# A list scheduler that gets TensorE's work in runs, at other prices

## The chip, the cores and the metric

The kernel runs on one core of a Trainium2 chip. Its engines are TensorE (PE in the profile; its weight loads are PEld), VectorE (DVE), ScalarE (ACT), GpSimd (POOL) and SyncE (SP), which issues the DMAs. Each engine works through its own instructions in order. The metric is the device time of one execution in microseconds, as the median of three runs.

## The reference

Two transformer blocks of two layers each on 256 tokens of width 1024, in float32. The first block has a gated delta rule beside an mLSTM in its first layer (`mixer_ab`) and windowed attention in its second (`mixer_c`), each followed by a feed-forward with squared relu of width 4096 and a gated per-layer input. The second block has five attentions side by side in each layer and a gated feed-forward of width 2816 with a short convolution:

```python
for layer in range(DEPTH):                       # first block
    mix = mixer_ab(hn, ...) if layer % 2 == 0 else mixer_c(hn, ...)
    h = h + rmsnorm(mix, gains[1])
    ff = jnp.square(jax.nn.relu(hn @ w_up[layer])) @ w_down[layer]
    h = h + rmsnorm(ff, gains[3])
    h = h + jax.nn.sigmoid(h @ w_ple_gate[layer]) * (p[layer] @ w_ple[layer])
...
for l in range(DEPTH):                           # second block
    mixed = jnp.concatenate([_merge(o_a), ..., _merge(o_e)], axis=-1)
    x = x + mixed @ w_o[l]
    x = x + (jax.nn.silu(gate) * (xn @ ffn_w_up[l])) @ ffn_w_down[l]
```

## The kernel before, in words

**Products in three passes.** A float32 product is made of three float32r products: high part of the activations times high part of the weights, and the two mixed products with a low part. `block` loads a weight block of 1 MB by DMA into a `raw` tile (two buffers) and splits it into `hi` and `lo` (four buffers each) in four parts: `hi` is a copy on ACT or DVE, `lo` is a subtraction on DVE.

**Two forms.** `tmm` (line 748) has the weights stationary and 256 tokens moving: for each of 2 channel groups and 8 k-tiles three matmuls of 256 columns, 48 for a block, all into one PSUM bank. `nmm` (line 760) has the activations stationary (one of two token tiles) and 512 columns of weights moving; for one k-tile and two banks it gives the six matmuls pass by pass, the two banks alternating:

```python
for i, b in enumerate(banks):
    pe.matmul(b[:, :n], a[0], hi[:, i * n : (i + 1) * n], start=first, stop=False)
for i, b in enumerate(banks):
    pe.matmul(b[:, :n], a[0], lo[:, i * n : (i + 1) * n], start=False, stop=False)
for i, b in enumerate(banks):
    pe.matmul(b[:, :n], a[1], hi[:, i * n : (i + 1) * n], start=False, stop=last)
```

In a feed-forward `tmm` makes the hidden units of block u, and `nmm` adds those of block u-1 into four banks that stay open (24 matmuls for a block: two token tiles, two k-tiles, two banks, three passes). There are 16 such blocks in each layer of the first block and 11 in each of the second, where `tmm` runs twice for a block. `transposes` (line 870) puts 2 to 4 transposes of 128x128 into one bank.

**The planner.** Nothing is issued as the program names it. `Recorder.note` (line 335) takes each instruction down as an `Op` with its price and with the instructions that it must follow because their data overlap; for PSUM a whole bank counts as one piece, so that matmuls into a bank keep their order. `price` (line 378) gives a time in ns by engine and size. For PE it is 118 for a transpose, 2 + 0.417 n for n columns of float32r or bfloat16, and 2 + max(1.67 n, 212) for float32. `arrange` (line 454) then lays the instructions out in time with these prices: at each step the engine that can start first gets, among what it can start first, the instruction with the highest rank, that is, the longest way to the end by `tails` (line 400). A tile of a pool is taken ahead of its turn only where the program's own order still fits. `order` (line 428) goes through seven such layouts and keeps the one with the shortest planned time. `issue` (line 568) emits the instructions in that order; every engine's queue follows from it. All instructions in the profile therefore carry line 571. Which of two engines makes a copy (ACT or DVE) or a column operation (POOL or DVE) is also decided in `arrange`, by what can end sooner.

A norm's factor is computed by `rsqrt_of` on POOL and DVE in a chain of small steps; `to_aT` transposes normed rows and splits them into `aTh` and `aTl`, which all following products read.

Of the kernel before, what the change touches and what calls it, by code (L numbers as in the profile page):

```python
# [36 lines left out]
# ---------------------------------------------------------------- layout of small inputs  # L37
# [35 lines left out]
# ---------------------------------------------------------------- constants of the shapes  # L73
# [66 lines left out]
def layout(x):  # L140
# [64 lines left out]
    def setk(name, g, n):  # L205
        """the gain of n heads below each other; of keys, one column for each head alone"""
        if COLS[name][1] == 1:
            return setc(name, np.tile(g, n))
        z = np.zeros((n, g.size, n), f32)
        for i in range(n):  # L210
            z[i, :, i] = g
        setc(name, z.reshape(P, n))
# [43 lines left out]
class Op:  # L256
    __slots__ = ("eng", "call", "args", "kwargs", "cost", "lag", "preds", "succs", "tiles", "table", "rank", "alt")
# [9 lines left out]
class Recorder:  # L267
    """Takes the program's instructions down in the order in which it names them, and issues them in another:
    each engine gets, of what can start first, the instruction with the longest way to go. Every order of two
    instructions on overlapping data is kept, and a pool's tile is taken ahead of its turn only if the  # L270
    program's own order still fits into the pool from there on."""
# [8 lines left out]
    def __init__(self, nc):  # L280
        self.engines = {"pe": nc.tensor, "act": nc.scalar, "dve": nc.vector, "pool": nc.gpsimd, "sp": nc.sync}
        self.ops, self.pools, self.tile_pool, self.seen = [], {}, {}, {}

    # ---------------------------------------------------------------- taking down
# [9 lines left out]
    def new(self, pool, bufs, tile):  # L294
        """a tile of a pool that is used again"""
# [4 lines left out]
    def either(self, first, second):  # L300
        """an instruction for the engine that can do it sooner; (engine, call, operands, keywords) each"""
# [7 lines left out]
    def copy(self, out, src, scale=1.0):  # L309
        """out = scale * src on ScalarE or VectorE"""  # L310
# [6 lines left out]
    def scalar(self, *args, **kwargs):  # L317
        """tensor_scalar of a column on GpSimd or VectorE"""
        self.either(("pool", "tensor_scalar", args, kwargs), ("dve", "tensor_scalar", args, kwargs))

    def box(self, x):
        """(tile, partitions, columns) of an operand; None if it isn't on the chip"""
# [12 lines left out]
    def note(self, eng, call, args, kwargs):  # L335
        op = Op()
        op.eng, op.call, op.args, op.kwargs = eng, call, args, kwargs
        op.preds, op.succs, op.tiles, op.alt = {}, [], [], None
# [8 lines left out]
        i = len(self.ops)  # L347
# [4 lines left out]
        self.ops.append(op)  # L352
# [25 lines left out]
    def price(self, op, out, ins):  # L378
        """a rough time in ns"""
# [4 lines left out]
        if op.eng == "pe":  # L384
            if op.call == "transpose":
                return 118
            n = _size(ins[1])
            return 2 + 0.417 * n if ins[1].dtype in (F32R, BF16) else 2 + max(1.67 * n, 212.0)
# [10 lines left out]
    # ---------------------------------------------------------------- putting in order  # L399
    def tails(self, starts):  # L400
        """each instruction's time to the end when the program is laid out from its end backwards"""
# [44 lines left out]
    def swap(self, op):  # L446
        """the other form of an instruction"""
# [6 lines left out]
    def arrange(self):  # L454
# [33 lines left out]
        p0, gone, out = 0, [False] * n, []  # L488
        by_rank, top = sorted(range(n), key=lambda i: -ops[i].rank), 0
        while len(out) < n:  # L490
# [4 lines left out]
            for e, cand in avail.items():  # L495
                pick = None
                for i in cand:
# [8 lines left out]
                    ok = True  # L506
                    for t in op.tiles:
                        if t not in taken:
                            p = pool[t]
                            room = self.pools[p] - (KEEP.get(p, 0) if op.rank < lead - SLACKTIME else 0)  # L510
                            if first[t] > p0 and use[p][p0 : first[t]].max() >= room:
                                ok = False
                                break
                            at = max(at, min(s[e] for s in slots[p]))
# [29 lines left out]
            for t in op.tiles:  # L544
                p = pool[t]
                if t not in taken:
# [21 lines left out]
    def issue(self):  # L568
        for i in self.order():
            op = self.ops[i]  # L570
            getattr(self.engines[op.eng], op.call)(*op.args, **op.kwargs)  # L571


class Loom:
    """Chains of dependent steps, each taken as far as what it needs is there."""
# [36 lines left out]
    def until(self, ready, *keys):  # L612
        """within a chain: wait for keys in ready"""
# [5 lines left out]
def program(ctx, tc, A, out, dbg=None):  # L619
# [64 lines left out]
    # ------------------------------------------------------------ resident data  # L684
# [33 lines left out]
    def pick(row):  # L718
        """as lhsT: that row of the moving operand on every output partition"""
        return ident[:, row : row + 1].to_broadcast([P, P])  # L720

    # ------------------------------------------------------------ weights
    def block(name, i, k, w):
        """block i of a packed weight: high and low parts [P, k, w]"""
# [11 lines left out]
    def whole(name, i, k, w):  # L736
        """block i of a packed weight as it is, for float32 products: four passes, but nothing to prepare"""
# [9 lines left out]
    # ------------------------------------------------------------ matrix products  # L747
    def tmm(bank, hi, lo, n=2):
        """bank[:, j, tokens] = (channel group j of the block)^T @ aT"""
        for j in range(n):  # L750
            c = ts(j)
            o = bank[:, j, :]
            for k in range(8):
                pe.matmul(o, hi[:, k, c], aTh[:, k, :], start=(k == 0), stop=False)
                pe.matmul(o, hi[:, k, c], aTl[:, k, :], start=False, stop=False)
                pe.matmul(o, lo[:, k, c], aTh[:, k, :], start=False, stop=(k == 7))
                if k % 4 == 3:
                    loom.step()

    def nmm(banks, a, hi, lo, first, last, n=512):  # L760
        """banks (column halves of n) += act^T @ W for one k-tile"""
        for i, b in enumerate(banks):
            pe.matmul(b[:, :n], a[0], hi[:, i * n : (i + 1) * n], start=first, stop=False)
        for i, b in enumerate(banks):
            pe.matmul(b[:, :n], a[0], lo[:, i * n : (i + 1) * n], start=False, stop=False)
        for i, b in enumerate(banks):
# [1315 lines left out]
```

## Time and profile before

| | |
|---|---|
| median of 3 runs | 1451.15 us (1449.95 to 1454.01) |
| span of the profiled execution | 1450.2 us |
| PE busy | 1401.3 us (97%), 8856 matmuls |
| PEld / DVE / ACT / POOL busy | 1239.8 / 1000.2 / 796.1 / 199.9 us |
| mean granted clock of PE | 0.994 of full speed |
| DMA | 236.40 MB, 163 GB/s in the mean |

The span is from the first to the last instruction. Busy time is the time in which an engine works at one instruction at least. A matmul's duration in the profile includes its passage through the array; matmuls follow each other faster than that, so their pace is read from starts that follow each other. A row of several instructions shows the time from the first start to the last end. A window counts an instruction that reaches into it from before as well.

### The profile page before, as it was taken

What the parts mean: (1) busy time and instruction counts of PE and PEld (TensorE: products, weight loads), DVE (VectorE), ACT (ScalarE), POOL (GpSimd) and SP (SyncE); (2) the same over time, 40 slices, a digit from 0 to 9 for tenths busy, and PEclk for the clock granted to TensorE, in tenths of its full rate; (3) what the DMA queues carried; (4) which work ended last, traced back from release to release, by engine and by line L of the source; (5) the groups of instructions that cost most, each with busy time, mean ns of one, the idle gap of its engine ahead of it and who ended that gap; (6) DMA issues with size and microseconds to landing.
All of it is one profiled execution on the core that took longest, in us unless ns stands there. A gap on an engine that the chain in (4) does not pass through costs nothing.

```text
span 1450.2 us, 23721 instructions
## 1 busy us (share of the span) xinstructions
PE 1401.3 (97%) x8856; PEld 1239.8 (85%) x8868; DVE 1000.2 (69%) x2320; ACT 796.1 (55%) x1810; POOL 199.9 (14%) x607
## 2 busy tenths in 40 slices
PE   7999999999999989999998999999999999999998
PEld 6899879999788879998786788999997778799997
DVE  6986776555778666556888766676567685656664
ACT  5554555444556635445575875564447586455543
POOL 0000530000110130000136412000004631100000
PEclk9999999999999999999999999999999999999999
DMA  8521344554553444545454222555544421345553
GB/s 331 190 88 59 116 172 166 209 193 177 208 191 126 158 160 166 212 175 213 146 206 170 108 103 88 204 203 180 198 157 174 149 103 59 118 166 182 184 196 115
DMA packets 36116, 236.40 MB, mean 163 GB/s; under 512 B 4128, under 2 KB 4384, under 8 KB 9888
## 3 DMA queue, kind: packets, MB, share of 16 engines
q1 hardware_dynamic: 36000, 234.88, 44.6%
q8 instruction: 70, 1.15, 0.3%
q14 instruction: 46, 0.38, 0.1%
HBM read 233.81 MB, written 1.05 MB: 162 GB/s over the span
## 4 chain that ended last, share of the span: by engine, by line
PE 76%; DVE 9%; POOL 9%; ACT 4%; issue 2%; DMA 0%; ACTq 0%; POOLq 0%; DVEq 0%
PE ps L571 76%; POOL s L571 9%; ACT w L571 3%; DVE w L571 3%; DVE s L571 2%; DVE lo L571 2%; DVE h L571 1%; DVE aTl L571 0%; DMA h<-in_x 0%; ACT hi L571 0%; ACT L571 0%; DVE tab L571 0%; ACT aTh L571 0%; ACT s L571 0%; DVE hi L571 0%
## 5 line engine op out<-in xcount | busy, mean ns | idle before, releaser
L571 ACT ACTIVATE hi<-raw 128x512 fp32r<-128x512 f32 (+1 forms) x789 | 436.7, 622 | 289.2 <-PE ps L571 241.6
L571 DVE TENSOR_TENSOR lo<-raw,hi 128x512 fp32r<-128x512 f32 (+2 forms) x836 | 522.2, 679 | 86.6 <-ACT hi L571 79.5
L571 PE MATMUL ps<-hi,w 128*128 128x512 f32 (+1 forms) x1272 | 390.6, 401 | 0.8 <-ACT w L571 0.6
L571 PE MATMUL ps<-aTh,hi 128*128 128x256 f32 x1256 | 327.6, 281 | 0.2 <-ACT aTh L571 0.2
L571 PE MATMUL ps<-aTh,lo 128*128 128x256 f32 x1256 | 323.7, 281 | 1.3 <-DVE lo L571 1.3
L571 PE MATMUL ps<-aTl,hi 128*128 128x256 f32 x1256 | 323.8, 281 | 0.7 <-DVE aTl L571 0.7
L571 PEld LDWEIGHTS ps<-hi,w 128*128 128x128 f32 x1272 | 222.0, 188 | 35.5 <-issue 1.9
L571 PEld LDWEIGHTS ps<-aTh,hi 128*128 128x128 f32 x1256 | 229.3, 189 | 11.1 <-ACT aTh L571 1.1
L571 PEld LDWEIGHTS ps<-aTh,lo 128*128 128x128 f32 x1256 | 227.7, 189 | 10.5 <-DVE lo L571 1.5
L571 PEld LDWEIGHTS ps<-aTl,hi 128*128 128x128 f32 x1256 | 226.9, 189 | 8.7 <-DVE aTl L571 1.0
L571 ACT ACTIVATE w<-ps 128x512 f32<-128x512 f32 (+4 forms) x260 | 131.3, 536 | 139.8 <-PE ps L571 133.4
L571 PE MATMUL ps<-lo,w 128*128 128x512 f32 (+1 forms) x620 | 202.6, 394 | 0.0
L571 PE MATMUL ps<-hi,aTh 128*128 128x512 f32 (+2 forms) x480 | 164.1, 373 | 4.1 <-DVE w L571 3.0
L571 PE MATMUL ps<-lo,aTh 128*128 128x512 f32 (+2 forms) x480 | 163.2, 370 | 4.9 <-DVE lo L571 4.9
L571 PE MATMUL ps<-hi,aTl 128*128 128x512 f32 (+2 forms) x480 | 162.8, 370 | 0.4 <-DVE aTl L571 0.3
L571 PE MATMUL ps<-w,w 128*128 128x128 f32 (+5 forms) x992 | 156.0, 286 | 1.3 <-DVE w L571 0.6
L571 POOL TENSOR_SCALAR s<-s 128x1 f32<-128x1 f32 (+6 forms) x222 | 78.2, 353 | 551.7 <-DVE s L571 294.0
L571 PEld LDWEIGHTS ps<-w,w 128*128 128x128 f32 (+1 forms) x992 | 139.2, 191 | 14.5 <-ACT w L571 2.7
L571 PE MATMUL ps<-cf,w 128*128 128x128 f32 (+1 forms) x612 | 115.3, 285 | 28.4 <-DVE w L571 23.6
L571 ACT ACTIVATE w<-w 128x512 fp32r<-128x512 f32 (+5 forms) x146 | 77.4, 538 | 109.4 <-DVE w L571 106.8
L571 PEld LDWEIGHTS ps<-cf,w 128*128 128x128 f32 (+1 forms) x612 | 81.8, 150 | 50.4 <-issue 18.5
L571 DVE CAST hi<-raw 128x512 fp32r<-128x512 f32 (+1 forms) x47 | 20.0, 425 | 151.5 <-PE ps L571 151.5
(101 smaller groups left out, 1348.6 us busy)
## 6 DMA issues: line engine op xcount, KB each, us to landing
raw<-in_wu SPq DMA_DIRECT2D x32, 1024.0 KB, 4.8
raw<-in_wd SPq DMA_DIRECT2D x32, 1024.0 KB, 5.4
raw<-in_fg SPq DMA_DIRECT2D x22, 1024.0 KB, 4.8
raw<-in_fu SPq DMA_DIRECT2D x22, 1024.0 KB, 4.8
raw<-in_fd SPq DMA_DIRECT2D x22, 1024.0 KB, 4.9
raw<-in_wi SPq DMA_DIRECT2D x20, 1024.0 KB, 4.8
raw<-in_w0t SPq DMA_DIRECT2D x10, 1024.0 KB, 4.8
raw<-in_wo SPq DMA_DIRECT2D x10, 1024.0 KB, 4.8
```

The source lines that it names most:

```text
L571: getattr(self.engines[op.eng], op.call)(*op.args, **op.kwargs)
```

## The change

No operation is added or taken out. `together` opens a run: the first instruction noted in it becomes an `Op` of the planner, and the following ones are added to it (`more`), with their price, what they must follow and their tiles. The planner places the run as one piece, from the time when everything that any of its instructions needs is there, and `issue` emits its instructions one behind the other. Runs are made for PE alone: six matmuls of two k-tiles in `tmm`, the three passes of one k-tile into one bank in `nmm` (the banks no longer alternate pass by pass), and all transposes of a bank. The prices of PE change: 109 for a transpose, 1 + 0.4414 n for float32r, 3 + 0.417 n for bfloat16, max(224, 2 + 1.68 n) for float32. In `arrange` an instruction that takes several new tiles of one pool now asks for room for all of them, and the search for a full pool is remembered between steps (`crowded`). Comments are taken out all over the file, so lines move.

```diff
+    @contextmanager
+    def together(self):
+        self.run = []
+        yield
+        self.run = None
...
         op.cost, op.lag = self.price(op, outs[-1], rest + ins), self.LAG[eng]
-        i = len(self.ops)
+        if self.run:
+            i = self.run[0]
+            first = self.ops[i]
+            first.more.append((call, args, kwargs))
+            first.cost += op.cost
+            op = first
+        else:
+            i = len(self.ops)
+            self.ops.append(op)
+            if self.run is not None:
+                self.run.append(i)
...
             if op.call == "transpose":
-                return 118
+                return 109
             n = _size(ins[1])
-            return 2 + 0.417 * n if ins[1].dtype in (F32R, BF16) else 2 + max(1.67 * n, 212.0)
+            if ins[1].dtype == F32R:
+                return 1 + 0.4414 * n
+            return 3 + 0.417 * n if ins[1].dtype == BF16 else max(224.0, 2 + 1.68 * n)
...
+        def crowded(p, room):
+            k = full[p].get(room)
+            if k is None or k < p0:
+                v = use[p][p0:n] >= room
+                k = p0 + int(v.argmax())
+                if k < n and not v[k - p0]:
+                    k = n
+                full[p][room] = k
+            return k
...
-                            if first[t] > p0 and use[p][p0 : first[t]].max() >= room:
+                            k = more.get(p, 0)
+                            more[p] = k + 1
+                            if k >= len(slots[p]) or first[t] > p0 and crowded(p, room - k) < first[t]:
                                 ok = False
                                 break
-                            at = max(at, min(s[e] for s in slots[p]))
+                            at = max(at, sorted(s[e] for s in slots[p])[k] if k else min(s[e] for s in slots[p]))
...
     def issue(self):
         for i in self.order():
             op = self.ops[i]
-            getattr(self.engines[op.eng], op.call)(*op.args, **op.kwargs)
+            for call, args, kwargs in [(op.call, op.args, op.kwargs)] + op.more:
+                getattr(self.engines[op.eng], call)(*args, **kwargs)
...
     def tmm(bank, hi, lo, n=2):
...
-            for k in range(8):
-                pe.matmul(o, hi[:, k, c], aTh[:, k, :], start=(k == 0), stop=False)
-                pe.matmul(o, hi[:, k, c], aTl[:, k, :], start=False, stop=False)
-                pe.matmul(o, lo[:, k, c], aTh[:, k, :], start=False, stop=(k == 7))
-                if k % 4 == 3:
+            for k0 in range(0, 8, 2):
+                with rec.together():
+                    for k in (k0, k0 + 1):
+                        pe.matmul(o, hi[:, k, c], aTh[:, k, :], start=(k == 0), stop=False)
+                        pe.matmul(o, hi[:, k, c], aTl[:, k, :], start=False, stop=False)
+                        pe.matmul(o, lo[:, k, c], aTh[:, k, :], start=False, stop=(k == 7))
+                if k0 % 4 == 2:
                     loom.step()
...
     def nmm(banks, a, hi, lo, first, last, n=512):
         for i, b in enumerate(banks):
-            pe.matmul(b[:, :n], a[0], hi[:, i * n : (i + 1) * n], start=first, stop=False)
-        for i, b in enumerate(banks):
-            pe.matmul(b[:, :n], a[0], lo[:, i * n : (i + 1) * n], start=False, stop=False)
-        for i, b in enumerate(banks):
-            pe.matmul(b[:, :n], a[1], hi[:, i * n : (i + 1) * n], start=False, stop=last)
+            c = slice(i * n, (i + 1) * n)
+            with rec.together():
+                pe.matmul(b[:, :n], a[0], hi[:, c], start=first, stop=False)
+                pe.matmul(b[:, :n], a[0], lo[:, c], start=False, stop=False)
+                pe.matmul(b[:, :n], a[1], hi[:, c], start=False, stop=last)
...
     def transposes(srcs):
         b = wk(4)
-        for i, s in enumerate(srcs):
-            pe.transpose(b[: s.shape[-1], i, :], s, ident)
+        with rec.together():
+            for i, s in enumerate(srcs):
+                pe.transpose(b[: s.shape[-1], i, :], s, ident)
         return b
```

## Rows read from the trace of the kernel before

**Rows 1.** Busy us (instructions) by stretch: PE, PEld, DVE, ACT, POOL, clock, DMA.

```profile
375.00:520.00 145.00, 137.04 (x714) 112.17 (x716) 110.34 (x264) 91.38 (x246) 25.05 (x46) 0.98 0.46 162
...
700.00:905.00 205.00, 192.75 (x1038) 159.45 (x1039) 154.56 (x455) 136.04 (x360) 72.23 (x225) 0.99 0.37 131
905.00:1090.00 185.00, 185.00 (x1340) 173.99 (x1339) 120.87 (x216) 93.76 (x178) 0.00 (x0) 1.00 0.52 186
1090.00:1300.00 210.00, 198.20 (x1197) 171.57 (x1201) 143.08 (x396) 132.33 (x347) 61.07 (x210) 0.98 0.35 124
...
sum 1450.20, PE 1401.34 PEld 1239.76 DVE 1000.19 ACT 796.09 POOL 199.92; mean PE 155.70 PEld 137.75 DVE 111.13 ACT 88.45 POOL 22.21
```

**Rows 2.** Waits of PE: who for whom, us in total, times, longest.

```profile
PE ps L571 <- DVE w L571: 27.9, 20, 8.0
PE ps L571 <- DVE lo L571: 6.2, 4, 2.6
```

**Rows 3.** Timeline of PE at 516 us: start, us, instruction, count, idle before.

```profile
516.13 2.13 PE L571 MATMUL ps<-cf,w 128*128 128x128 f32 x8 [5.99 <-DVE w L571]
```

**Rows 4.** Timeline of all engines, 790 to 794 us.

```profile
790.19 0.73 PE L571 MATMUL ps<-hi,aTh 128*128 128x512 f32 x2 [0.50 <-ACT hi L571]
...
791.02 0.43 DVE L571 TENSOR_TENSOR w<-w,s 128x256 f32<-128x256 f32 x1 [1.16 <-POOL s L571]
...
793.57 0.79 PE L571 MATMUL ps<-lo,aTh 128*128 128x512 f32 x1 [2.65 <-DVE lo L571]
```

**Rows 5.** Busy time and clock just behind that stall.

```profile
793.50:796.90 3.40, 3.33 (x8) 2.66 (x9) 3.40 (x12) 1.15 (x2) 1.42 (x3) 0.50 0.23 43
```

**Rows 6.** Busy time in windows: PE on 512 columns alone, on 256 alone.

```profile
680.00:698.00 18.00, 18.00 (x81) 14.92 (x80) 13.40 (x26) 11.63 (x24) 0.34 (x1) 1.00 0.69 254
909.00:919.00 10.00, 10.00 (x90) 10.00 (x90) 3.39 (x7) 1.20 (x3) 0.00 (x0) 1.00 0.58 211
```

**Rows 7.** PE's groups by shape: count, busy us, mean ns of one, idle before.

```profile
L571 PE MATMUL ps<-hi,w 128*128 128x512 f32 x1256 | 386.5, 402 | 0.8 <-ACT w L571 0.6 <-DVE w L571 0.2
L571 PE MATMUL ps<-aTh,hi 128*128 128x256 f32 x1256 | 327.6, 281 | 0.2 <-ACT aTh L571 0.2
...
L571 PE MATMUL ps<-lo,w 128*128 128x512 f32 x612 | 200.1, 395 | 0.0
L571 PE MATMUL ps<-hi,aTh 128*128 128x512 f32 x320 | 119.6, 411 | 4.1 <-DVE w L571 3.0 <-ACT aTh L571 0.6 <-ACT hi L571 0.5
...
L571 PE MATMUL ps<-cf,w 128*128 128x128 f32 x580 | 110.0, 284 | 27.7 <-DVE w L571 22.9 <-DVE s L571 3.5 <-ACT w L571 1.0
```

**Rows 8.** Timeline of DVE: four splits of weights, and one alone.

```profile
502.21 2.50 DVE L571 TENSOR_TENSOR lo<-raw,hi 128x512 fp32r<-128x512 f32 x4
...
783.87 0.68 DVE L571 TENSOR_TENSOR lo<-raw,hi 128x512 fp32r<-128x512 f32 x1
```

**Rows 9.** Timeline of PE: four transposes in a row, and two set apart.

```profile
473.96 0.61 PE L571 MATMUL ps<-cf,w 128*128 128x128 f32 x4
...
503.37 0.27 PE L571 MATMUL ps<-cf,w 128*128 128x128 f32 x1
503.40 0.71 PE L571 MATMUL ps<-hi,w 128*128 128x512 f32 x2
503.95 0.27 PE L571 MATMUL ps<-cf,w 128*128 128x128 f32 x1
```

**Rows 10.** Timeline of PE: first, some and last changes between widths.

```profile
38.59 1.02 PE L571 MATMUL ps<-hi,w 128*128 128x512 f32 x2
...
267.86 0.63 PE L571 MATMUL ps<-hi,w 128*128 128x512 f32 x2
268.32 0.40 PE L571 MATMUL ps<-aTh,lo 128*128 128x256 f32 x2
268.56 0.39 PE L571 MATMUL ps<-aTh,hi 128*128 128x256 f32 x2
268.79 0.63 PE L571 MATMUL ps<-lo,w 128*128 128x512 f32 x2
...
1432.70 1.07 PE L571 MATMUL ps<-hi,w 128*128 128x512 f32 x4
```

More of the change, by code (lines that the diff above doesn't have):

```diff
@@ L1 @@
 import math
-from contextlib import ExitStack
+from contextlib import ExitStack, contextmanager
 import numpy as np
@@ L256 @@
 class Op:
-    __slots__ = ("eng", "call", "args", "kwargs", "cost", "lag", "preds", "succs", "tiles", "table", "rank", "alt")
+    __slots__ = ("eng", "call", "args", "kwargs", "cost", "lag", "preds", "succs", "tiles", "table", "rank", "alt", "more")
 def _size(ap):
@@ L282, in __init__ @@
         self.ops, self.pools, self.tile_pool, self.seen = [], {}, {}, {}
+        self.run = None
[3 more added lines that the diff above has]
+        yield
+        self.run = None
     def engine(self, name):
@@ L337, in note @@
         op.eng, op.call, op.args, op.kwargs = eng, call, args, kwargs
-        op.preds, op.succs, op.tiles, op.alt = {}, [], [], None
+        op.preds, op.succs, op.tiles, op.alt, op.more = {}, [], [], None, []
         op.table = self.TABLES.get(args[2], 0) if call == "activation" and args[2] != AF.Copy else None
@@ L351, in note @@
                 self.touch(i, op, b, write)
-        self.ops.append(op)
     def touch(self, i, op, b, write):
@@ L488, in arrange @@
         p0, gone, out = 0, [False] * n, []
+        full = {p: {} for p in self.pools}
+        def crowded(p, room):
[7 more added lines that the diff above has]
+            return k
         by_rank, top = sorted(range(n), key=lambda i: -ops[i].rank), 0
@@ L505, in arrange @@
                         continue
-                    ok = True
+                    ok, more = True, {}
                     for t in op.tiles:
@@ L545, in arrange @@
                 p = pool[t]
+                if t not in taken or left[t] == 1:
+                    full[p].clear()
                 if t not in taken:
```

## The prediction

> **What bounds the kernel now.** I read the busy time by stretch first [rows 1]. TensorE (PE) is busy 1401.34 of 1450.20 us, so 48.9 us are idle. The reader is to see that this idle time is not spread evenly: the feed-forward stretch 905-1090 us has none (185.00 of 185.00), while three stretches with mixers (attention and its projections) hold 145.00-137.04 = 8.0, 205.00-192.75 = 12.3 and 210.00-198.20 = 11.8 us, together 32 us. The rest lies at the start and the end. So the bound is PE's own stream, except in the mixers, where dependent chains through the other engines run out of cover. Second, the table of who waited for whom [rows 2]: PE's waits are put down to VectorE (DVE), 27.9 us on working tiles and 6.2 us on the low parts of weights. Third, two places of the timeline. At 509.9-516.1 PE stands 5.99 us for one transpose [rows 3]; it has nothing else to do while a norm's chain goes through GpSimd (POOL). An order of PE's work does not shorten that chain. At 790-793.6 it is otherwise [rows 4]: DVE stands 1.16 us at the head of its queue for a POOL result, the split of weights is queued behind, and PE waits 2.65 us for that split. That is a wrong order of DVE's work against PE's, and so the kind of stall that a better plan can take away. After this stall the granted clock is half, 0.50 over 793.5-796.9 us [rows 5]: the lower of PE's two levels, 1.2 GHz.
>
> **The change, part by part.** It adds and removes no instruction. It alters the order on all engines, by three means: PE's work is planned in runs that nothing may enter; a pair of banks is no longer alternated pass by pass but gets three passes each; and prices change.
>
> *Prices.* The planner has 215.5 ns for a product of 512 columns and 108.8 for 256. In 18.00 us with nothing else 81 products of 512 columns are counted, those that reach in from before among them (a duration of 0.402 us): 18.40/81 = 227 ns. For 256 columns it is 10.28/90 = 114 ns [rows 6, 7]. The new prices are 227 and 114. DVE, which the mixers' stalls hang on, was priced rightly: four splits stand in 2.50 us and one alone shows 0.68, so they follow each other after (2.50-0.68)/3 = 607 ns [rows 8], against 601 in the code. So PE was too cheap beside it: with 1256+612+3x320 = 2828 products of 512 columns and 3x1256 = 3768 of 256 [rows 7], 2828x11 + 3768x5 ns = 31 + 19 = 50 us, 3.6% of its busy time. In a feed-forward stretch this costs nothing, since PE is busy anyway. In a mixer it can put DVE's chain steps and weight splits in a wrong sequence, as at 790 us. What can come back is bounded by half of the 32 us, -16 (the rest being chains like the one at 510 us), and on the other side by the same kind of stall falling elsewhere: the two mixers of the second block are the same program in different company, and their idle differs by only 12.3-11.8 = 0.5 us, so +5 is wide. I take -4 us, two thirds of the 6.2 us that PE waits for weight splits [rows 2], the row nearest to this mechanism.
>
> The Trainium skill, page "TensorE: Matmul & The Clock Gate", section "Wait — 56ns, not 53.3ns?", speaks against this part: back-to-back products take columns / 2.4 GHz + about 2.5 ns, 215.7 ns for 512 columns, which is the old price. The trace does not agree (227 and 114 ns), and the measurement decides. By the page the old plan was right, this term would be 0 and the sum -2.5 us at best.
>
> *Transposes as one run.* A transpose alone between products costs 503.95-503.37 = 0.58 us less two products of 227 ns, 126 ns; in a run of four it is (0.61-0.284)/3 = 109 ns [rows 7, 9]. So 17 ns for each one set apart. If all 580 [rows 7] stood alone, 10 us; if all banks stood whole already, nothing. The rows show both. With about three to a bank there are some 200 banks; if every second one is torn once, 100x17 ns = 1.7. I take -1.5 us.
>
> *Runs of six and of three.* In an alternating stretch two products of 512 and four of 256 columns take 268.79-267.86 = 0.93 us [rows 10], against 2x227+4x114 = 910 ns in long runs: 10 ns for each of the two changes of width. The span has 661 changes, the first at 38.59 and the last at 1432.70 us [rows 10]: 6.6 us in all. After the change a feed-forward block has 48/6 = 8 runs of 256-column products and 24/3 = 8 runs of 512-column ones. If the kinds alternated run by run, 54 blocks (2x16 and 2x11) x 16 = 864 changes, +2 us; if the two banks of one k-tile, which have equal rank, stay together, 54x8 = 432, -2.3 us; all gone would be -6.6. I take -2 us, near the second: products come in pairs now too (the x2 of rows 10).
>
> *What is queued behind a run.* A run is planned only when its last operand is there. The chip issues the instructions singly, so at a stall like that at 790 us the first of them still runs ahead, but one product fewer (two ran ahead, rows 4): 0.23 us at each such stall. There are a few: +1 us. DMAs keep their order relative to the buffers they wait for; their share is not near a bound in the mixers (0.35 to 0.46, rows 1), so I cost their moves at 0, and if that cover goes, it appears as PE waiting for weight splits, which is in the bounds above.
>
> **Sum:** -4 -1.5 -2 +1 = -6.5 us, or 1443.7 for the profiled execution (1450.2 from first to last instruction). The median of the runs, 1451.15, is 0.95 above that span, so 1444.6 there.
>
> **The rivals.**
> *Much faster.* If a true price frees the whole bound of 16 us, with the 3.5 us of runs, and with the half-clock stretch of 3.4 us behind the 790 us stall, where half of the speed is lost (1.7 us), the time is 1451.15-16-3.5-1.7 = 1430. For it: all three mixers idle. Against: the largest single stall (5.99 us) is a chain that no order shortens.
> *No change.* PE is busy 97% of the time and the mixers' idle is dependent chains. Then only the runs' 1 or 2 us remain: 1450. For it: twin mixers with equal idle, which looks like a property of the chains rather than of the order.
> *A price that is wrong the other way.* If products elsewhere ran at the old price, the new one would be 50 us too dear where the old was right: PE's fill would be planned too long, DVE's splits too late, and the stalls for low parts (6.2 us, rows 2) would come a second time while the runs give 2.5: 1455. Against: both paces of rows 6 and the pair of rows 10 are at the new price. The page's rule named above would make it so.
> *Slower: coarse steps in the chains.* A step of a chain that needs PE in the mixers now waits behind half a run of three, 0.34 us, in place of half a product, 0.11; and a bank's transposes start only when the last of them can, 3x0.11 us later. That is 0.56 us at each hop. An attention has five hops (transposes before the scores, scores, transposes of the probabilities, product with the values, transposes of the result). If three attentions follow each other in each of the three mixer stretches (an estimate from the code), that is 3x3x5 = 45 hops, 25 us if all lay bare. For it: PE waits 27.9 us for DVE's working tiles, which are such hops. Against: most hops have other PE work beside them, busy being 94% there (528.0 of 560 us). It decides from the point where about a third of the hops (7.5 us, what the other parts give) are exposed; with two thirds, 17 us, the time is 1451+17-7.5 = 1460.
>
> **How the numbers follow.** A run of this kernel repeats within about 0.3% (4.4 us); less than that counts as the same. The forecast, 1439 to 1449 by its own terms, has 0.42; much faster 0.13; no change 0.20; the wrong price 0.02; coarse steps 0.23. Faster by over 0.3% (below 1446.8): 0.36 of the forecast and 0.13, together 0.49. Within: 0.06 of the forecast, 0.20 of no change, 0.01 of the wrong price, 0.27. Slower: 0.01 of the wrong price and 0.23, 0.24. The range reaches to the fast rival's time and just past the slow one's, which leaves out half of each, 0.18: 1430 to 1461. The likeliest case alone keeps its own ten microseconds.
>
> **What would show it.** Right: idle PE of the three mixer stretches falls from 32 to about 28 us, with the wait for DVE's low parts falling from 6.2 to 2 or so; PE's busy time falls by 3 or 4 us; transposes stand in rows of two to four; the feed-forward stretch keeps no idle. The price term is wrong if the wait for low parts stays; the run term if busy time does not fall, or the products' pace moves away from 227 and 114 ns. The slower rival shows in PE's wait for DVE's and ACT's working tiles rising well above 27.9 us with idle in the mixers over 40. The prediction as a whole is wrong if the time moves by more than 15 us either way.

## The result and the profile after

The changed kernel is slower: 1477.09 us in the median (1474.91 to 1479.16) against 1451.12, a ratio of 1.0175 [1.0155, 1.0194]. The forecast was 1444.6 and the range ended at 1461. The profiled execution spans 1477.2 us, 27.0 more.

The page's first lines of the kernel after, busy time and share of each engine:

```profile
span 1477.2 us, 23739 instructions
PE 1411.3 (96%) x8858; PEld 1257.7 (85%) x8868; DVE 1011.4 (68%) x2350; ACT 777.4 (53%) x1779; POOL 190.3 (13%) x606
```

PE's idle time is 1477.2-1411.3 = 65.9 us, 17.0 more than the 48.9 of before; its busy time grew by 10.0. Busy time by stretch, after, in the columns of [rows 1] and at the same stages, which now lie 10 to 25 us later:

```profile
385.00:535.00 150.00, 138.45 (x723) 115.18 (x725) 113.30 (x270) 86.69 (x237) 25.04 (x51) 0.95 0.42 151
710.00:925.00 215.00, 198.93 (x1060) 167.80 (x1062) 159.15 (x470) 135.38 (x359) 63.69 (x222) 0.97 0.35 125
925.00:1115.00 190.00, 190.00 (x1364) 178.70 (x1364) 126.01 (x230) 96.65 (x187) 4.40 (x10) 1.00 0.53 185
1115.00:1325.00 210.00, 192.91 (x1149) 168.58 (x1151) 139.20 (x385) 122.10 (x323) 63.17 (x204) 0.96 0.33 119
```

The three stretches with mixers hold 11.6 + 16.1 + 17.1 = 44.7 us of idle PE, where [rows 1] had 32; the feed-forward stretch still has none. The clock column fell from 0.98, 0.99, 0.98 to 0.95, 0.97, 0.96: the records of the granted clock that end within the span show half of full speed, the 1.2 GHz level, over 48 us, against 17 before. Products of 512 columns start 427 ns after each other there and 227 elsewhere (medians of the trace after). In these stretches PE was busy for 40.0 us, against 14.3; about half of the difference, 13 us, is speed lost. So the 10.0 us more of busy time are some +13 from the clock and a remainder of -3, and 17 + 13 - 3 = 27.

The waits, after (who for whom, us in total, times, longest), beside [rows 2]:

```profile
PE ps L608 <- DVE w L608: 41.8, 21, 8.4
DVE w L608 <- POOL s L608: 33.3, 21, 3.8
DVE s L608 <- POOL s L608: 19.1, 33, 2.9
PE ps L608 <- ACT w L608: 7.6, 8, 2.2
PE ps L608 <- DVE h L608: 7.2, 4, 2.5
PE ps L608 <- DVE lo L608: 3.2, 3, 1.7
```

PE's wait for the low parts of weights fell from 6.2 to 3.2, the sign that the price term named; its wait for the working tiles of the chains rose from 27.9 to 41.8, and more beside it. One of these stalls, in the timeline of all engines of the kernel after (start, us, engine, instruction, count, idle before and who ended it):

```profile
1152.68 2.49 DVE L608 TENSOR_TENSOR lo<-raw,hi 128x512 fp32r<-128x512 f32 x4
1152.79 0.66 POOL L608 TENSOR_SCALAR s<-s 128x4 f32<-128x4 f32 x1
1153.42 0.61 POOL L608 TENSOR_TENSOR s<-s,s 128x4 f32<-128x4 f32 x1
1153.98 0.65 POOL L608 TENSOR_TENSOR s<-s 128x4 f32<-128x4 f32 x1
1154.59 0.67 POOL L608 TENSOR_SCALAR s<-s 128x4 f32<-128x4 f32 x1
1155.23 0.35 POOL L608 TENSOR_TENSOR s<-s,s 128x4 f32<-128x4 f32 x2
...
1156.59 0.22 POOL L608 TENSOR_SCALAR s<-s 128x4 f32<-128x4 f32 x1
1156.89 0.20 POOL L608 TENSOR_TENSOR s<-s 128x4 f32<-128x4 f32 x1
...
1158.31 0.42 DVE L608 TENSOR_TENSOR w<-w,s 128x256 f32<-128x256 f32 x1 [3.14 <-POOL s L608]
1158.36 0.45 POOL L608 TENSOR_SCALAR s<-s 128x4 f32<-128x4 f32 x1
...
1158.79 0.44 PE L608 MATMUL ps<-cf,w 128*128 128x128 f32 x2 [2.56 <-DVE w L608]
```

Read it from the bottom. PE stands 2.56 us for a transpose of a normed tile. DVE, which makes that tile, stands 3.14 us at the head of its queue for POOL. And POOL is in a chain of small steps that goes slowly just as long as DVE's four splits run beside it: from 1152.79 to 1155.23 four steps, 0.61 us each by their starts; from there to 1158.36, with DVE idle, 14 steps, 0.22 us each. The planner prices such a step at 162 (tensor_tensor) or 185 ns (tensor_scalar). Behind the stall the clock is halved (busy time of the window, after):

```profile
1160.50:1163.90 3.40, 3.40 (x10) 2.62 (x9) 2.28 (x8) 1.70 (x4) 2.91 (x10) 0.50 0.01 2
```

### The profile page after: what moved, and what is told of

Read it like the earlier page. It is cut to its first block, busy times and chain, and to the rows that moved or that the text cites. A ratio compares the mean times of both kernels' runs of the same rounds, so it can differ in the third digit from the quotient of the medians.

```text
span 1477.2 us, 23739 instructions
## 1 busy us (share of the span) xinstructions
PE 1411.3 (96%) x8858; PEld 1257.7 (85%) x8868; DVE 1011.4 (68%) x2350; ACT 777.4 (53%) x1779; POOL 190.3 (13%) x606
## 4 chain that ended last, share of the span: by engine, by line
PE 71%; DVE 11%; POOL 8%; ACT 5%; issue 2%; DMA 2%; ACTq 0%; POOLq 0%; SPq 0%
PE ps L608 71%; POOL s L608 8%; DVE w L608 4%; ACT w L608 4%; DVE lo L608 3%; DVE s L608 2%; ACT hi L608 1%; DMA raw<-in_w0t 1%; DVE h L608 1%; DMA raw<-in_wi 1%; DVE aTl L608 0%; DMA raw<-in_wm 0%; DMA h<-in_x 0%; DVE tab L608 0%; ACT L608 0%
## 5 line engine op out<-in xcount | busy, mean ns | idle before, releaser
L608 ACT ACTIVATE hi<-raw 128x512 fp32r<-128x512 f32 (+2 forms) x759 | 417.1, 620 | 319.7 <-PE ps L608 265.5
L608 PE MATMUL ps<-hi,w 128*128 128x512 f32 (+1 forms) x1272 | 426.4, 397 | 0.0
L608 PE MATMUL ps<-aTh,hi 128*128 128x256 f32 x1256 | 357.1, 284 | 2.2 <-ACT w L608 2.2
L608 PE MATMUL ps<-aTl,hi 128*128 128x256 f32 x1256 | 353.8, 282 | 0.7 <-DVE aTl L608 0.4
L608 PE MATMUL ps<-aTh,lo 128*128 128x256 f32 x1256 | 353.5, 281 | 0.7 <-DVE lo L608 0.7
L608 PE MATMUL ps<-lo,w 128*128 128x512 f32 (+1 forms) x620 | 241.0, 389 | 0.0
L608 PE MATMUL ps<-hi,aTh 128*128 128x512 f32 (+2 forms) x480 | 181.9, 379 | 6.9 <-DVE w L608 5.3
L608 DVE CAST hi<-raw 128x512 fp32r<-128x512 f32 x77 | 32.5, 426 | 201.4 <-PE ps L608 201.3
L608 PEld LDWEIGHTS ps<-lo,w 128*128 128x128 f32 x620 | 116.5, 188 | 18.9 <-DVE lo L608 0.2
L608 ACT ACTIVATE w<-w 128x512 f32<-128x512 f32 (+5 forms) x146 | 76.9, 536 | 88.1 <-DVE w L608 85.9
```

What stands on the lines that cost most here:

```text
L608: getattr(self.engines[op.eng], call)(*args, **kwargs)
```

## The experiments

Idle is span less PE's busy time. The half clock is the sum of the granted clock's records at half speed that end within the span. "DVE for POOL" is the sum of DVE's waits that POOL ended. All three are in us. "Landing" and "POOL" stand for the two prices that e9 corrects, "slope" for the factor of n in the price of a product, "transposes" for the runs of a bank's transposes.

| kernel | median us | ratio to before | idle PE | half clock | DVE for POOL |
|---|---|---|---|---|---|
| before | 1451 to 1453 | | 48.9 | 17 | 48 |
| after | 1477.1 | 1.0175 [1.0155, 1.0194] | 65.9 | 48 | 54 |
| e1 new prices, no runs | 1496.5 | 1.0308 [1.0293, 1.0324] | 74.8 | 55 | 50 |
| e2 runs at old prices | 1468.8 | 1.0118 [1.0101, 1.0135] | 58.0 | 51 | 45 |
| e3 transpose 119 | 1453.0 | 1.0008 [0.9999, 1.0017] | 47.8 | 27 | 36 |
| e4 after, pairs alternate | 1473.3 | 1.0145 [1.013, 1.016] | 63.4 | 38 | 54 |
| e5 float32r price alone | 1500.5 | 1.0335 [1.0313, 1.0356] | 77.0 | 38 | 51 |
| e6 transpose 109 alone | 1462.2 | 1.0075 [1.0057, 1.0094] | 52.0 | 27 | 48 |
| e7 slope 0.4455 | 1481.7 | 1.0211 [1.0195, 1.0226] | 65.8 | 48 | 43 |
| e8 slope 0.39 | 1446.3 | 0.9965 [0.9953, 0.9977] | 45.5 | 20 | 40 |
| e9 after + POOL + landing | 1450.9 | 0.999 [0.998, 1.0] | 44.0 | 34 | 14 |
| e10 e1 + POOL + landing | 1459.8 | 1.0049 [1.0034, 1.0064] | 50.0 | 34 | 20 |
| e11 e1 + POOL | 1483.2 | 1.021 [1.0191, 1.023] | 63.8 | 48 | 18 |
| e12 runs of six + POOL + landing | 1453.3 | 1.0003 [0.9993, 1.0012] | 48.9 | 31 | 21 |
| e13 e1 + landing | 1472.4 | 1.0132 [1.0119, 1.0146] | 62.4 | 34 | 49 |
| e14 before + POOL + landing | 1453.6 | 1.0008 [0.9999, 1.0017] | 48.8 | 38 | 18 |
| e15 slope 0.41, POOL, landing 1500, transposes | 1449.8 | 0.9972 [0.996, 0.9984] | 42.0 | 31 | 16 |
| e16 slope 0.39, POOL, transposes | 1444.1 | 0.9944 [0.993, 0.9957] | 43.3 | 14 | 14 |
| e17 e2 + POOL + landing | 1449.2 | 0.9979 [0.997, 0.9988] | 44.5 | 24 | 17 |
| e18 slope 0.40, POOL, runs of six, transposes | 1447.1 | 0.9957 [0.9942, 0.9973] | 39.7 | 31 | 13 |

**Which part lost it (e1 to e4).** e1 is before with the new prices and nothing else:

```diff
-                return 118
+                return 109
...
-            return 2 + 0.417 * n if ins[1].dtype in (F32R, BF16) else 2 + max(1.67 * n, 212.0)
+            if ins[1].dtype == F32R:
+                return 1 + 0.4414 * n
+            return 3 + 0.417 * n if ins[1].dtype == BF16 else max(224.0, 2 + 1.68 * n)
```

> The kernel before with the new prices of TensorE alone, no runs. Theory 1 (the prices do the harm: with dearer products the planner lays chains and weight splits out in a worse order): 1465 to 1480, idle TensorE 60 us or more. Theory 2 (the runs do it, coarse steps in the chains): 1440 to 1455, idle 44 to 52. Theory 3 (any small change of the plan scatters the time, neither part is the cause by itself): anywhere from 1445 to 1475, without adding up with the runs alone to +26.

e2 is the kernel after with the old prices, the same lines the other way round:

```diff
-                return 109
+                return 118
...
-                return 1 + 0.4414 * n
...
+            return 2 + 0.417 * n if ins[1].dtype in (F32R, BF16) else 2 + max(1.67 * n, 212.0)
```

> The changed kernel with the old prices: runs alone. Theory 1: 1440 to 1453. Theory 2: 1465 to 1480, idle TensorE over 60 us. Theory 3: somewhere from 1445 to 1475. In each the changes between widths are cheap as in the changed kernel (products of 512 columns at 227 ns all through).

e3 is before with a price moved by 1 ns, to see what a mere other order costs:

```diff
-                return 118
+                return 119
```

> The kernel before with the price of a transpose at 119 ns instead of 118 and nothing else: what order luck alone is worth. Theories 1 and 2: within 4 us of 1451. Theory 3: off by 5 us or more either way (a greedy planner takes other ways after the first tie that falls differently).

e4 is after without the runs of three:

```diff
-            with rec.together():
-                pe.matmul(b[:, :n], a[0], hi[:, c], start=first, stop=False)
-                pe.matmul(b[:, :n], a[0], lo[:, c], start=False, stop=False)
-                pe.matmul(b[:, :n], a[1], hi[:, c], start=False, stop=last)
+            pe.matmul(b[:, :n], a[0], hi[:, i * n : (i + 1) * n], start=first, stop=False)
+        for i, b in enumerate(banks):
+            pe.matmul(b[:, :n], a[0], lo[:, i * n : (i + 1) * n], start=False, stop=False)
...
```

> The changed kernel with its prices, where nmm has no runs and alternates the banks as before; tmm and the transposes keep their runs. Theory 1: 1470 to 1480, as the changed kernel. Theory 2, if the runs of nmm are the coarse steps that hurt: 1445 to 1458. If the runs of the transposes or of tmm hurt: 1470 or more.

The new prices alone cost 45 us, the runs alone 17, and both together 26: they don't add, and beside the runs the prices cost 8 (e2 to after). So neither part carries the 26 by itself. The nudge of e3 moved stalls about and the time by 1. e4, without the runs of three, keeps 22 of the 26, so it isn't these runs that hurt. e1 lies above the range of every theory, and e2 in that of theory 2, with 58 us of idle time where it said over 60.

**Which price, and is there a direction (e5 to e8).** Each is before with one price changed:

```diff
-            return 2 + 0.417 * n if ins[1].dtype in (F32R, BF16) else 2 + max(1.67 * n, 212.0)
+            if ins[1].dtype == F32R:
+                return 1 + 0.4414 * n
```

> Before, with the change's price for float32r products alone (1 + 0.4414 n for 2 + 0.417 n: 227 for 215.5 ns at 512 columns, 114 for 108.8 at 256); the transposes keep 118, everything else is as before, no runs. Theory A (dear products): the float32r price carries the loss of all the new prices (1496), so 1485 to 1500. Theory B (jumps: the list scheduler's order falls to a better or a worse one with any step of a price, and the old one is a good draw): any time from 1455 to 1495, with the stalls at other places than with all the new prices. Theory C (the transposes' price, 109 for 118, did the harm): 1450 to 1460.

```diff
-                return 118
+                return 109
```

> Before, with the change's price for transposes alone (109 for 118 ns), no runs. Theory A (dear products): within 0.3% of before, 1447 to 1456, since some 580 transposes by 9 ns are 5 us of 1400 and the price is lower, not higher. Theory B (jumps): slower by about 10 us, 1455 to 1470, with new stalls of 2 us and more. Theory C (transposes' price): 1485 to 1500.

```diff
-            return 2 + 0.417 * n
+            return 2 + 0.4455 * n
```

> Before, with one number changed: the slope of the products' price 0.4455 in place of 0.417, so 230 ns for 512 columns and 116 for 256, dearer than the change's own 227 and 114; no runs. Theory A (dear products): at least as slow as the float32r price alone, 1485 or more. Theory B (jumps): no direction in the price, 1450 to 1470, below the run with the float32r price.

```diff
-            return 2 + 0.417 * n
+            return 2 + 0.39 * n
```

> Before, with the slope 0.39 in place of 0.417: products too cheap, 201.7 ns for 512 columns and 101.8 for 256. Theory A (dear products; a too cheap price makes the planner do the chains early): no slower than before, 1440 to 1452. Theory B (jumps): slower, 1456 to 1475, as a step upwards of the same size is. If an accurate price were what matters (the forecast's premise), the time would rise with the distance from 0.4414: 1456 or more here, and less than before at 0.4414, which the runs so far contradict.

The float32r price carries the loss (1500 alone). There is a direction: the two dear products lose 30 and 49 us, and a price that is further from the trace on the cheap side gains 5. Beside it there are jumps of 10 to 20 us that follow no rule: 0.4455 is dearer than e5's and 19 us faster, between the ranges of theories A and B, and e6, a transpose that is cheaper and nearer to the trace, costs 10, where theory A had nothing.

**What stands beside the product's price (e9 to e13).** If a true price harms, another may be false beside it. Two are, by the trace. POOL's single-column steps are priced at 178 or 254 ns and show means of 513 and 546 in the kernel before; the others, of 2 to 16 columns, are priced at 157 to 215 ns and show means of 246 to 424 (three of its groups: count, busy us, mean ns of one, idle before):

```profile
L571 POOL TENSOR_SCALAR s<-s,s 128x1 f32<-128x1 f32 x69 | 37.6, 546 | 449.3 <-DVE s L571 278.0 <-ACT w L571 167.6 <-ACT hi L571 0.7
L571 POOL TENSOR_SCALAR s<-s 128x1 f32<-128x1 f32 x62 | 31.8, 513 | 275.5 <-ACT w L571 244.7 <-DVE s L571 26.9
L571 POOL TENSOR_TENSOR s<-s,s 128x4 f32<-128x4 f32 x60 | 14.5, 246 | 4.1
```

And a transfer of 1024 KB is priced at 2.92 us (2.87 and a fixed 0.05) with 0.91 until it has landed, 3.8 together; the row of the DMA issues (out<-in, count, size, median us to landing) of the kernel after says 4.8:

```profile
raw<-in_wu SPq DMA_DIRECT2D x32, 1024.0 KB, 4.8
```

Theory D: the plan, once products are dear, has chains and splits ready just in time by prices that are too low, and on the chip they come late; the old product, 5% too cheap, made PE late by as much, which hid it. e9 is the kernel after with both prices corrected:

```diff
-           "sp": dict.fromkeys(("pe", "act", "dve", "pool", "sp"), 910)}
+           "sp": dict.fromkeys(("pe", "act", "dve", "pool", "sp"), 2000)}
...
-            return 38 + 0.82 * n if op.call == "memset" else (152 if op.call == "tensor_tensor" else 175) + 2.5 * n + 76 * per_row
+            return 38 + 0.82 * n if op.call == "memset" else 290 if op.call == "tensor_tensor" else (400 if n == 1 else 265) + 60 * per_row
```

> The changed kernel with two more prices from the trace: GpSimd (POOL) 400 ns for a tensor_scalar of one column and 265 for more, +60 with a per-row operand, 290 for a tensor_tensor (it had 152 to 254; the trace shows means of 513 and 546 for one column, 246 to 345 for the others), and a transfer's landing 2000 ns after its price (it had 910: 1024 KB are priced at 2.87 us and land after 3.8, where the trace shows a median of 4.8). Theory D (half a correction: the dearer product was true, but the steps beside it, POOL's and the DMA's, stayed too cheap, so the plan lets the chains begin just in time and on the chip they are late; the old product, 5% too cheap, had hidden that): at least 20 of the 26 us come back, 1440 to 1458, and PE's waits for working tiles fall from 41.8 + 7.6 towards 30. Theory A (a dear product is bad by itself): 1470 or more. Theory B (jumps without direction): 1455 to 1490.

All of the 26 us come back. The waits of e9, in the lines that stand above for the kernel after:

```profile
PE ps L608 <- DVE w L608: 25.7, 13, 8.2
DVE s L608 <- POOL s L608: 8.7, 16, 1.3
DVE w L608 <- POOL s L608: 5.3, 9, 1.6
PE ps L608 <- DVE lo L608: 3.0, 4, 1.5
```

PE's wait for working tiles fell from 41.8 to 25.7 and DVE's for POOL from 33.3 + 19.1 to 14.0. e10, e11 and e13 are e1 with both prices, POOL's alone and the landing's alone, the lines of e9's diff. For e10 and e11, of which e10 has the landing's line too:

```diff
-                return 118
+                return 109
...
+                return 1 + 0.4414 * n
...
+            return 38 + 0.82 * n if op.call == "memset" else 290 if op.call == "tensor_tensor" else (400 if n == 1 else 265) + 60 * per_row
```

> The new product prices without runs (1496) and with the same two prices for POOL and the landing. Theory D: 35 or more of the 45 us come back, 1440 to 1462. Theory A: 1485 or more. Theory B: 1455 to 1500.

> The new product prices without runs and with POOL's price alone; the landing stays at 910. Theory D with POOL as the main gap (the norms' chains run through it, and its steps are priced at half of what they take): 1460 to 1475, most of the way back. With the landing as the main gap: 1485 to 1500. Theory A: 1485 or more.

For e13:

```diff
-           "sp": dict.fromkeys(("pe", "act", "dve", "pool", "sp"), 910)}
+           "sp": dict.fromkeys(("pe", "act", "dve", "pool", "sp"), 2000)}
```

> The new product prices without runs (1496) with the true landing of a transfer alone (2000 ns for 910); POOL's price stays as it was. With POOL's price alone it was 1483, with both 1460. If the landing is the larger gap, it gives most of the 37 us by itself: 1455 to 1472, and DVE's waits for POOL stay near the 48 us they are now (28.7 + 18.2 + 1.2 before). If the two only help together: 1480 to 1495.

The square is complete: 1496 with neither, 1483 with POOL's price (-13), 1472 with the landing (-24), 1460 with both (-37), so beside the new product prices the two add. I had expected POOL to be the main gap; the landing is the larger one, and e11 lies between the ranges of the two cases. What each repairs is told by place. POOL's price takes DVE's waits for POOL from 50 to 18 us and leaves a stall at 95 us; the landing leaves the waits at 49 and removes that stall. Busy time in the window 90 to 105 us of e1, of e11 and of e13:

```profile
90.00:105.00 15.00, 7.33 (x20) 4.84 (x20) 7.12 (x38) 2.67 (x7) 0.00 (x0) 0.56 0.34 133
```

```profile
90.00:105.00 15.00, 7.34 (x20) 4.85 (x20) 7.39 (x49) 2.73 (x7) 0.00 (x0) 0.58 0.36 137
```

```profile
90.00:105.00 15.00, 15.00 (x135) 15.00 (x134) 13.91 (x73) 5.73 (x10) 0.00 (x0) 1.00 0.20 71
```

20 matmuls in 15 us against 135: in e1 and e11 PE has no weight products in its queue while the first mixer's chain is not ready, and the clock is at half for most of it. Three lines of e1's timeline speak against a late transfer as the cause at this place:

```profile
89.63 2.49 DVE L573 TENSOR_TENSOR lo<-raw,hi 128x512 fp32r<-128x512 f32 x4
94.67 2.07 PE L573 MATMUL ps<-w,cf 128*128 128x256 f32 x4 [6.13 <-ACT w L573]
121.44 0.37 PE L573 MATMUL ps<-aTh,hi 128*128 128x256 f32 x1
```

The last split of weights ends at 92.12, PE stands for the chain until 94.67, and it takes weight products up again at 121.44, with no split between. The weights were there; PE's order has them behind the chain. So the landing's price acts here through the order that it makes. By which steps of the plan it avoids the stall was not followed further.

e12 is e9 without the runs of three and of transposes:

```diff
-            with rec.together():
-                for i, s in enumerate(srcs):
-                    pe.transpose(b[: s.shape[-1], i, :], s, ident)
+            for i, s in enumerate(srcs):
+                pe.transpose(b[: s.shape[-1], i, :], s, ident)
...
```

> The changed kernel with the runs of six alone (a bank of aT products), nothing else in runs, the new product prices, and the two prices for POOL and the landing. Theory D: the best of these, 1436 to 1452, since all prices are near the trace, the runs of six save changes of width, and the pairs of banks still alternate. Theory A: 1470 or more. Theory B: 1450 to 1490.

It is 2 us slower than e9 and 1 past its range, not the best: with the prices mended, these runs cost nothing.

**Did the cheap product hide it (e14), and are the runs coarse (e17)?** e14 is before with both prices of e9 and the cheap product kept; e17 is e2 with both.

```diff
-           "sp": dict.fromkeys(("pe", "act", "dve", "pool", "sp"), 910)}
+           "sp": dict.fromkeys(("pe", "act", "dve", "pool", "sp"), 2000)}
...
+            return 38 + 0.82 * n if op.call == "memset" else 290 if op.call == "tensor_tensor" else (400 if n == 1 else 265) + 60 * per_row
```

> Before, with its cheap products kept (215.5 ns) and POOL's price and the landing corrected; no runs. Theory D says that the cheap product hid the cheap steps beside it, so correcting these brings little where the product is cheap: 1443 to 1458, within 10 us of before, against the 37 us that the same two prices gave beside dear products. If POOL's price and the landing are simply good by themselves: 1425 or less. DVE's waits for POOL fall from 48 to about 20 us in either case.

> The run with the change's three kinds of runs at the old product prices (1469, 17 above before), with POOL's price and the landing corrected. If the runs themselves cost those 17 us (coarse steps in the chains), they stay: 1463 to 1475. If the runs only made the order more exposed to the same two prices (theory D also for the runs): 1440 to 1456, as with the new product prices (1451).

Beside cheap products the same two prices bring nothing (1453.6), although DVE's waits for POOL fall from 48 to 18 us: taking those waits away won no time here. That PE itself is late enough to hide them is theory D's reading and not shown. And the 17 us of the runs alone vanish (1449.2): the runs had no cost of their own either, they only exposed the order to the same two prices. All eight combinations, in us:

| | old prices of POOL and landing | both corrected |
|---|---|---|
| prices and order of before (before, e14) | 1451.6 | 1453.6 |
| new product prices (e1, e10) | 1496.5 | 1459.8 |
| runs (e2, e17) | 1468.8 | 1449.2 |
| both (after, e9) | 1477.1 | 1450.9 |

In the left column the four kernels lie 45 us apart, in the right one 11. Jumps like e5's against e7 could make one such pair; that all four on the right lie within 9 us of before speaks for the two prices. There the new product prices still gain nothing (+6 without runs, +2 with them), and the runs are 4 and 9 us faster, the sign that the forecast gave them. Whether the two prices must be true or only dearer wasn't tried: no run has them overdone.

**Forwards (e15, e16, e18).** If slack is what counts, products should be cheap and the steps beside them dear. Three kernels differ in slope, runs and landing; e16, the fastest, against before:

```diff
-            return 2 + 0.417 * n
+            return 2 + 0.39 * n
...
+            return 38 + 0.82 * n if op.call == "memset" else 290 if op.call == "tensor_tensor" else (400 if n == 1 else 265) + 60 * per_row
...
+            with rec.together():
+                for i, s in enumerate(srcs):
```

> A try at a kernel that beats before: slope 0.41 (products a little cheaper still), POOL's price as the trace has it, a landing of 1500 ns, and a bank's transposes as one run; the products alternate as before. Theory D: product cheap and steps beside it dear, so chains early: 1435 to 1448. Theory B (jumps): 1445 to 1470.

> A second try: slope 0.39 (1446 by itself), POOL's price as the trace has it, the landing at 910, a bank's transposes as one run. Theory D: 1435 to 1447, no slower than the slope 0.39 by itself. Theory B: 1445 to 1470.

> A third try at a faster kernel: slope 0.40, POOL's price as the trace has it, the landing at 910, the runs of six and a bank's transposes as one run, the two banks of a pair alternating. Theory D: 1435 to 1447; if the runs of six save what the sum gave them (changes of width), a few us below the second try (1444). Theory B: 1445 to 1470.

e16, 1444.1 us, beats both kernels (0.9944 [0.993, 0.9957] of before); PE's wait for working tiles is 18.5 us and the half clock 14. e15 missed its range by 2 us, and e18, at the end of its own, shows no gain from the runs of six over e16. With the slope of 0.39 alone e8 is at 1446.3, so most of e16's gain may be that slope's. Between orders of such kernels a few us are left that the theory doesn't tell.

## Why the prediction was wrong

- **The step that failed is the price term, -4 us with "+5 is wide" as its other end.** Alone it measures +45 (e1), nine times the worst that I allowed it, and beside the runs +8 (e2 to after). Its observation was right (PE too cheap, 227 for 215.5 ns), its inference was not: "DVE, which the mixers' stalls hang on, was priced rightly ... So PE was too cheap beside it". I compared PE's price with one other engine. The mixers' chains also go through POOL, whose steps take more than three times their price beside splits, and a transfer lands 1 us later than priced; [rows 4] had the POOL wait in plain view. With these two prices corrected as well the new product prices cost 2 to 6 us in place of 8 to 45 (e9, e10, e14 and e17). That the cheap product had been the slack that hid the two false prices fits the eight kernels of the table, but no run follows it through the plan. The gain of 4 is seen nowhere.
- **The runs' terms failed too: -2, -1.5 and +1, together -2.5 us, measure +17 at the old prices (e2).** They were priced by what PE does inside a run; for what coarser pieces do to the order around them the sum had the +1 alone. With POOL's price and the landing corrected the 17 vanish (e17), so these two stand behind this loss as well. And the sum added the two parts, which don't add: 45 and 17 alone, 26 together.
- **What of the runs held is the count.** Changes of width between products of 512 and 256 columns fell from 661 to 236, and transposes that start right behind another rose from 333 to 438 of 580, by the traces: 425x10 + 105x17 ns = 6 us by [rows 9, 10], where the forecast had 3.5. That PE's busy time fell by it is not shown. It rose by 10, which the forecast had named as a sign against this term, and with the time lost to the clock taken out 3 are left; but the same reckoning gives 1388 us (e14) and 1403 us (e5) for kernels without any runs, 1394 for before and 1391 for after, so 3 us are within what other orders do.
- **The bound was taken from the idle time that was there.** Half of 32 us limits what can be gained, not what can be lost: e1 has 26 us more idle time than before. Twin mixers with nearly equal idle said nothing about other plans.
- **The low parts.** Predicted from 6.2 to about 2, measured 3.2. It is no proof of the price's mechanism: with the new product price and no runs this wait is 7.8 us (e1), 2.4 (e5) or, with 0.4455, 10.2 (e7).
- **The rival on the slow side, coarse steps (1460, 0.23),** had the sign and the mark (waits for working tiles "well above 27.9 us with idle in the mixers over 40": 41.8 and 44.7), but not the cause: with the same runs e9 and e17 are at 1451 and 1449. Its price, 0.56 us for each hop, is not seen there.
- **The clock** had 1.7 us in one rival and nothing in the sum. It was some 13 of the 27: 17 us more of idle time came with 13 us lost at the 1.2 GHz level. This is no fixed ratio: in e5, by the same reckoning, 28 us more of idle time came with 7.
- **The stall of 5.99 us that no order shortens** stood (it begins at 510.1, not 509.9). In the kernel after:

```profile
525.06 2.12 PE L608 MATMUL ps<-cf,w 128*128 128x128 f32 x8 [5.67 <-DVE w L608]
```

Still open: how the 26 us of the whole change divide between POOL's price and the landing (only e1's 37 were divided), how the landing's price changes the order, and the jumps among orders at like prices (e5 against e7, e6).

## What to carry to other kernels

In a list scheduler one price acts together with all others: here one was corrected alone, and the time rose by 45 us; with two more corrected the loss shrank to 8. Before a price is mended, hold the price of every engine on the chains against the trace, transfers to their landing included, and mend them together. That gave back what was lost here and no more. The fastest kernel here keeps a price that is too low on the busiest engine; that this works as slack for the other engines is the reading that fits, not one that was followed in a plan.

## What the runs showed of the hardware

POOL's small steps depend on what DVE does: 0.61 us each beside splits, 0.22 with DVE idle, in one chain. Over the whole trace of the kernel after, steps of two columns or more that lie wholly beside splits last 700 ns in the mean (39 of them), those with DVE idle 214 ns (196). ScalarE doesn't matter to them: with DVE idle they last 216 ns beside its work and 213 without, over the traces of before, after, e1 and e9. The Trainium skill, page "GPSIMD Engine Reference", section "1. Specifications", says that GpSimd's way to SBUF is shared with VectorE and contended by VectorE instructions with two SBUF inputs, which a split (`lo` from `raw` and `hi`) is; this trace agrees, with the numbers above. So no single price is right for POOL here; the 265 and 290 ns that e9 gives these steps lie between the two cases.
